# Decoder trunk on one core: kernel zeros sent later, x splits at high priority, one gate tile ahead of the GLU, and a pause between scan tiles

## The chip, the cores and the metric

The kernel runs on one core of a Trainium2 chip. The metric is the device time of one launch in microseconds, the median of the runs. TensorE is called PE here, its weight load PEld, VectorE DVE, ScalarE ACT, GpSimd POOL, and the engine that issues most transfers SP.

## The reference

Two layers are applied to x of 512 tokens by 1024 channels, in float32. Each layer projects x once and splits the columns:

```
proj = x @ w_in[l]     # 1024 -> u 512 | z_ssm 512 | q latent 256 | kv latent 128 | rotary key 32
                       #         | z_mla 512 | q_mem 512 | z_mem 512 | merge-gate logits 3 x 1024
y_ssm = glu(s5(u)) * silu(z_ssm)              # 32 groups x 64 complex states, scan over 512 tokens
y_mla = latent_attention(...) * silu(z_mla)   # 8 heads, causal, rotary part of 32
y_mem = attention(q_mem, mem) * silu(z_mem)   # 4 heads, 256 memory tokens
merged = sum_i sigmoid(gate_i) * (y_i @ p_i)  # 1024 channels
x = layer_norm(ALPHA * x + merged @ w_out[l])
glu(y): g = gelu(y); a, b = split(g @ w_glu + b_glu); a * sigmoid(b)
```

The S5 branch discretises a diagonal state matrix with a step `dt = exp(log_dt)` per group, so exponentials, sines and cosines of the parameters are needed before its scan.

## The kernel before

**Matmuls.** Everything is kept transposed, channels on partitions and the 512 tokens as columns. Float32 accuracy comes from splitting each operand into a rounded high half and a remainder: `split_to` casts the high half on ACT (L594, or L597 with a scale) and subtracts it on DVE (L595, L598). `mm3` then issues three matmuls, high by high (L97), high by low (L98) and low by high (L99). `w_in_tile` makes one 128-column tile of the input projection: two weight blocks (`wblock`: a load of 256 KB by SP, a cast, a subtract) and 24 matmuls of 512 columns. `gate2` makes of such a tile z times 1 + tanh(z/2): a tanh on ACT and a multiply on DVE.

**Order.** PE's instructions run in the order in which the Python generators issue them. A running model of PE time, `E.clk`, advanced by each `mm3`, decides when a background stream (`tick`) gets its turn. The other engines' instructions are ordered by a scheduler by priority; `tc.high_priority` moves instructions forward. Each engine executes its list strictly in order, and so does SP's list of transfers.

**Start of layer 0.** `first_tiles` loads the weights of three latent tiles and the eight tiles of x (`x(k)`), and multiplies as they arrive. `param_setup` computes on DVE `dt` by `v_exp` (some 20 small operations, L109 to L124), then on POOL the phases (`v_sincos` on `ang = ai * dt`, L299), and from these all S5 parameters; the second `v_exp` (mag) is again on DVE. POOL goes on with `s5_powers` and `s5_pool` of scan tile 0, which makes `bt`, `bm`, `cl`, `cosn` and `sinn`; POOL's tensor operations have the line of a helper, L71. Meanwhile PE makes u tile 0, u tile 1, the rotary key, `mem_values` and `mem_keys`.

**The scan stream.** `s5_stream` runs four tiles of eight groups per layer as background. `s5_tile` issues: `kp`, the convolution kernel of a block of 8 tokens (L477, L478); two transposes of `bm`; `pb` = B u; on DVE a rotation with `cosn` and `sinn` (L513 to L518), a scan (L519), and the rotation back; then `py`, a GELU, a transpose `yt` back (L540), a copy of it on ACT (L542), and two transfers through DRAM that end in `yb`. The next tile or the end of the stream splits `yb` (L597, L598 in `tail`) into one of four operands `E.g` of the GLU. `kp`, `tp`, `pb`, `py` and `yt` share one PSUM bank. The kernel tile `kt` is written into the middle of a DRAM buffer `E.kd` whose front 112 columns are zeros, so that it can be read back as a Toeplitz matrix `tz`. These zeros are stored once, at the start of the program.

**Around the stream.** In each layer the memory attention runs first (scores `sm`), then eight merge tiles of that branch, then up to four gate tiles of the S5 branch (`ZS`, each only while the stream is not done), then what is left of the stream, then `glu_tile` 0 to 2. `mla_phase` runs the eight heads of the latent attention with fill work between the steps: GLU tile 3, then for every even head the gate tile `ZA` of that pair of heads and two merge tiles. `mla_values` transposes the probabilities (L963), copies them (`pt`, L966) and multiplies by v (`av`, L971). The buffers of the pool F (five) hold the tanh results, gates and GLU intermediates.

Of the kernel before, what the change touches and what calls it, by code (L numbers as in the profile page):

```python
# [10 lines left out]
F32 = mybir.dt.float32  # L11
# [443 lines left out]
    E.uds[ut] = ud  # L455


def s5_tile(E, l, ut, t, tail):

    nc = E.nc
# [8 lines left out]
    kd = E.kd[ut % 2]  # L471
# [85 lines left out]
def s5_stream(E, l, first, period):  # L557

    base = E.clk + first
    tail = None  # L560
    for ut in range(4):
        t = E.s5t if E.s5t is not None else s5_pool(E, l, ut)
        E.s5t = None
        yield max(base + ut * period, E.clk)
        tile = s5_tile(E, l, ut, t, tail)
        while True:
            try:
                d = next(tile)
            except StopIteration as e:
                tail = e.value  # L570
                break
            yield E.clk + d
    yield E.clk + E.cfg["tok_us"]
    tail()
# [88 lines left out]
def first_tiles(E, l):  # L663

    n = 3
    ps = [pmm(E) for _ in range(n)]
    E.X = [[E.xp.tile([128, 4, 512], F32R, name="X", tag="X") for _ in range(2)] for _ in range(2)]

    def x(k):
        raw = load_raw(E, E.I["xT"][k], tag="PPPPPPFF"[k])  # L670
        split_to(E, *xpart(k), raw)

    def xpart(k):
        return tuple(a[:, k % 4, :] for a in E.X[k // 4])

    def mm(t, k):
        mm3(E, ps[t], w[t].at(cols(k % 4)), xpart(k), k == 0, k == 7)

    src = lambda t, hf: E.I["w_in"][l, Tiles.CQ + t, hf]
    w = [wblock(E, src(0, 0))]  # L680
    x(0)
    mm(0, 0)
    w.append(wblock(E, src(1, 0)))
    mm(1, 0)
    x(1)
    mm(0, 1)
    w.append(wblock(E, src(2, 0)))
    mm(1, 1)
    x(2)
    mm(2, 0)  # L690
    mm(2, 1)
    x(3)
    for t in range(n):
        mm(t, 2)
    w2 = [split(E, load_raw(E, src(t, 1), tag="S")) for t in range(n)]
    x(4)
    for t in range(n):
        mm(t, 3)
    load_params(E)
    w = w2  # L700
    for k in range(4, 8):
        if k > 4:
            x(k)
        for t in range(n):
            mm(t, k)
    return ps
# [94 lines left out]
def latents(E, l):  # L801

    nc = E.nc
    v = nc.vector
    cs, sq = [], []
    first = first_tiles(E, l) if l == 0 else None
    for i, t in enumerate((Tiles.CQ, Tiles.CQ + 1, Tiles.CKV)):
        ps = first[i] if first else (yield from w_in_tile(E, l, t))
        c = ftile(E, "c")
        v.tensor_copy(c, ps)  # L810
        s = stile(E, "sq")
        nc.scalar.activation(out=s, in_=ps, func=AF.Square)
        cs.append(c)
        sq.append(s)
    if l == 0:
        param_setup(E)
    yield from u_tile(E, l, 0)
    if l == 0:
        mem_load(E, "AAAA")
        yield from u_tile(E, l, 1)  # L820
    ss = E.psum.tile([128, 512], F32, name="ss", tag="sc")
    v.tensor_tensor(out=sq[0], in0=sq[0], in1=sq[1], op=ALU.add)
    for j in range(2):
        for t in range(4):
            nc.tensor.matmul(ss[32 * t:32 * t + 32, cols(j)], lhsT=E.ones, rhs=sq[2 * j][:, cols(t)], start=True, stop=True)
    m2, hu = stile(E, "ms"), stile(E, "hu")
    ms, rs = m2[:, 0:256], m2[:, 256:512]
    for j, n in enumerate((256, 128)):
        v.tensor_scalar(out=ms[:, cols(j)], in0=ss[:, cols(j)], scalar1=1.0 / n, scalar2=EPS, op0=ALU.mult, op1=ALU.add)
    v_rsqrt(nc, rs, ms, hu[:, 0:256], hu[:, 256:512])  # L830
    if l > 0:
        yield from u_tile(E, l, 1)
    pk = pmm(E)
    w = load_raw(E, E.I["w_kr"][l], 256)
    for k in range(2):
        for b in range(2):
            for i in range(4):
                x = (k * 4 + i) * 32
                nc.tensor.matmul(pk[32 * i:32 * i + 32, :], lhsT=w[:, x:x + 32], rhs=fl(E.X[k][b][:, i, :]),
                                 start=k + b == 0, stop=k + b == 2)  # L840
    E.ks = stile(E, "ks") if l else E.cst.tile([128, 512], F32, name="ks", tag="cs")
    nc.scalar.copy(E.ks, pk)
    E.clk += 3.4
    yield
    if l == 0:
        E.phases = s5_powers(E, l)
        next(E.phases)
        yield from mem_values(E, l)
    E.cn = []
    E.scale = scale_latents(E, l, cs, rs)  # L850
    if l > 0:
        drain(E.scale)
        rotate_key(E, rotary_sums(E))
# [140 lines left out]
def z_tile(E, l, t, box, pool=None):  # L994
    box.append(gate2(E, (yield from w_in_tile(E, l, t)), pool))
# [177 lines left out]
def run(E, gen):  # L1173
    for _ in gen:
        tick(E)
# [114 lines left out]
    run(E, f)  # L1290


def mla_phase(E, l, first, fill):

    ys, ks, vs, ws, qs, z = {}, {}, {}, {}, {}, {}

    def prepare(h):
        hp, j = h // 2, h % 2
        if j == 0:
            ks[hp] = yield from mla_k(E, l, hp)  # L1300
            ws[hp] = wblock(E, E.I["w_uq"][l, hp])
            z[hp] = []
        qs[h] = yield from mla_q(E, l, hp, j, ws[hp])
        if h in (0, 3):
            vs[(h + 1) // 4] = yield from mla_v(E, l, (h + 1) // 4)

    def values(h, Ps, f):
        hp, j = h // 2, h % 2
        if j == 0:
            ys[hp] = E.yp.tile([128, 512], F32, name="ya", tag="Y")  # L1310
        return mla_values(E, h, Ps, vs[h // 4], ys[hp], z[hp], f)

    def fills(h):
        if h >= 0 and h % 2 == 0:
            return [z_tile(E, l, Tiles.ZA + h // 2, z[h // 2])] + fill[h:h + 2]
        return [first] if h < 0 else []

    f = attention(E, HEADS, prepare, lambda h, Ps: mla_scores(E, qs[h], ks[h // 2][h % 2], Ps), values, fills, E.cfg["mla_lag"],
                  E.cfg["mla_us"], E.cfg["lace_us"])
    run(E, f)  # L1320
    E.ya = [split(E, ys[hp], 0.5) for hp in range(4)]
# [9 lines left out]
def trunk(tc, I, out):  # L1331
    nc = tc.nc
    with ExitStack() as es:
# [15 lines left out]
        E.clk, E.bg, E.bg_at, E.s5t, E.uds = 0.0, None, 0.0, None, [None] * 4  # L1349
        E.x1 = E.dram.tile([S, D], F32, name="x1", tag="x1", bufs=1)  # L1350
        es.enter_context(tc.manual_schedule(engines={mybir.EngineType.PE}))
        zk = E.s5b.tile([128, 1024], F32, name="zk", tag="tz")
        nc.gpsimd.memset(zk, 0.0)
        E.kd = []
        for i in range(2):
            E.kd.append(E.dram.tile([32, 8, 240], F32, name="kd", tag=f"kd{i}", bufs=1))
            for h in range(2):
                nc.sync.dma_start(out=E.kd[i][0:16, :, h * 56:h * 56 + 56], in_=zk[0:16, 0:448].rearrange("p (g x) -> p g x", g=8))
        for l in range(DEPTH):
            E.macc, E.mg, E.g, E.ym, E.ysm = [None] * 8, [], [], [], []  # L1360
            if l == 0:
                warm_up(E)
            run(E, latents(E, l))
            E.bg = s5_stream(E, l, CFG["s5_first"][l], CFG["s5_period"])
            E.bg_at = E.clk
            tick(E)
            if l == 0:
                for i, _ in enumerate(mem_keys(E, l)):
                    if i in E.cfg["sl"]:
                        next(E.scale, None)  # L1370
                    tick(E)
            mem_phase(E, l)
            ym = [split(E, y, 0.5) for y in E.ym]
            rope = rope_tables(E) if l == 0 else idle()
            next(rope, None)
            for m in range(8):
                run(E, merge_tile(E, l, 2, m, ym, True, False))
                if m < 4:
                    next(rope, None)
            if l == 0:  # L1380
                ps = rotary_sums(E)
                drain(rope)
                rotate_key(E, ps)
            z = [[] for _ in range(4)]
            for i in range(CFG["zs"]):
                if E.bg is not None:
                    run(E, z_tile(E, l, Tiles.ZS + i, z[i], "P"))
            while E.bg is not None:
                E.bg_at = 0.0
                tick(E)  # L1390
            run(E, chain(*[glu_tile(E, l, i, z[i]) for i in range(3)]))
            mla_phase(E, l, glu_tile(E, l, 3, z[3]), [merge_tile(E, l, 0, m, E.ysm, False, False, E.halting) for m in range(8)])
            if l + 1 < DEPTH:
                E.phases = s5_powers(E, l + 1)
                next(E.phases)
                E.s5t = s5_pool(E, l + 1, 0)
            run(E, merge_all(E, l, 1, E.ya, False, True))
            run(E, out_norm(E, l, I["x"] if l == 0 else E.x1, out if l == DEPTH - 1 else E.x1))
# [75 lines left out]
```

## Time and profile before

| | |
|---|---|
| median of 3 runs | 1124.85 us (1123.71 to 1125.21) |
| profiled execution | 1121.5 us |
| its span, first to last instruction | 1119.4 us |
| mean granted PE clock | 0.985 of full speed |
| PE / PEld / DVE / ACT / POOL busy | 95% / 76% / 62% / 45% / 45% |
| DMA | 117.97 MB, 105 GB/s |

A matmul is pipelined, so its busy time (0.39 us for 512 columns) is longer than the distance to the next one. Idle time in brackets is what an engine waited just before an instruction, with the engine and line that released it.

### The profile page before, as it was taken

What the parts mean: (1) busy time and instruction counts of PE and PEld (TensorE: products, weight loads), DVE (VectorE), ACT (ScalarE), POOL (GpSimd) and SP (SyncE); (2) the same over time, 40 slices, a digit from 0 to 9 for tenths busy, and PEclk for the clock granted to TensorE, in tenths of its full rate; (3) what the DMA queues carried; (4) which work ended last, traced back from release to release, by engine and by line L of the source; (5) the groups of instructions that cost most, each with busy time, mean ns of one, the idle gap of its engine ahead of it and who ended that gap; (6) DMA issues with size and microseconds to landing.
All of it is one profiled execution on the core that took longest, in us unless ns stands there. A gap on an engine that the chain in (4) does not pass through costs nothing.

```text
span 1119.4 us, 16046 instructions
## 1 busy us (share of the span) xinstructions
PE 1063.0 (95%) x5584; PEld 851.8 (76%) x5584; DVE 695.2 (62%) x1274; ACT 508.7 (45%) x1010; POOL 499.5 (45%) x890
## 2 busy tenths in 40 slices
PE   7979999999999999999979999899899999999995
PEld 5678777777877777888868788788788777778885
DVE  7686687964666663753586676675447565545328
ACT  4335544233576654433334355433346656543331
POOL 4998885661033334863550275581002243320163
PEclk9989999999999999999999999999999999999998
DMA  6534244253322222444544434344322222234341
GB/s 197 150 115 123 69 113 119 77 146 88 86 70 67 68 76 67 134 121 134 151 144 140 116 97 109 94 118 120 103 83 88 73 52 74 67 115 130 111 134 76
DMA packets 87665, 117.97 MB, mean 105 GB/s; under 512 B 24097, under 2 KB 36513, under 8 KB 87585
## 3 DMA queue, kind: packets, MB, share of 16 engines
q1 hardware_dynamic: 86944, 114.85, 36.4%
q0 software_dynamic: 640, 2.10, 0.7%
q8 instruction: 44, 0.72, 0.3%
q14 instruction: 37, 0.30, 0.1%
HBM read 107.37 MB, written 9.55 MB: 104 GB/s over the span
## 4 chain that ended last, share of the span: by engine, by line
PE 64%; DVE 13%; POOL 9%; DMA 7%; ACT 3%; issue 3%; SPq 1%; DVEq 0%; ACTq 0%; POOLq 0%
PE mm L97 17%; PE mm L99 17%; PE mm L98 17%; PE av L971 2%; PE tp L963 2%; DMA raw<-in_w_in 2%; DMA yb<-yd 2%; DVE w L595 2%; DMA yd<-r 2%; POOL carve L71 1%; PE py L531 1%; POOL cl L71 1%; DMA raw<-in_w_out 1%; PE sa L98 1%; PE sa L99 1%
## 5 line engine op out<-in xcount | busy, mean ns | idle before, releaser
L97 PE MATMUL mm<-X,w 128*128 128x512 f32 x740 | 298.0, 403 | 0.6 <-ACT X L594 0.5
L99 PE MATMUL mm<-X,w 128*128 128x512 f32 x740 | 290.2, 392 | 2.2 <-DVE w L595 2.1
L98 PE MATMUL mm<-X,w 128*128 128x512 f32 x740 | 289.7, 391 | 0.2 <-DVE X L595 0.2
L595 DVE TENSOR_TENSOR w<-raw,w 128x512 fp32r<-128x512 f32 (+2 forms) x247 | 206.7, 842 | 123.0 <-ACT w L594 121.5
L594 ACT CAST w<-raw 128x512 fp32r<-128x512 f32 (+1 forms) x317 | 191.5, 606 | 193.5 <-PE mm L99 89.8
L71 POOL TENSOR_TENSOR w<-raw,w 128x512 fp32r<-128x512 f32 x70 | 92.9, 1329 | 316.2 <-ACT w L594 239.3
L99 PEld LDWEIGHTS mm<-X,w 128*128 128x128 f32 x740 | 139.2, 188 | 34.2 <-DVE w L595 3.9
L97 PEld LDWEIGHTS mm<-X,w 128*128 128x128 f32 x740 | 140.3, 190 | 30.6 <-issue 2.9
L98 PEld LDWEIGHTS mm<-X,w 128*128 128x128 f32 x740 | 139.6, 189 | 27.1 <-DVE X L595 0.9
L97 PE MATMUL mm<-hl,w 128*128 128x512 f32 (+1 forms) x296 | 112.9, 382 | 4.7 <-ACT hl L597 4.7
L99 PE MATMUL mm<-hl,w 128*128 128x512 f32 (+1 forms) x296 | 111.5, 377 | 5.9 <-DVE w L595 5.9
L98 PE MATMUL mm<-hl,w 128*128 128x512 f32 (+1 forms) x296 | 111.0, 375 | 1.3 <-DVE hl L598 1.3
L99 PEld LDWEIGHTS mm<-hl,w 128*128 128x128 f32 x296 | 57.5, 194 | 16.7 <-DVE w L595 7.0
L97 PEld LDWEIGHTS mm<-hl,w 128*128 128x128 f32 x296 | 57.6, 194 | 14.2 <-ACT hl L597 5.5
L98 PEld LDWEIGHTS mm<-hl,w 128*128 128x128 f32 x296 | 57.6, 195 | 10.7 <-DVE hl L598 1.9
L1029 ACT ACTIVATE thg<-mm,bg 128x512 f32<-128x512 f32 x48 | 33.0, 687 | 59.2 <-PE mm L99 57.1
L762 ACT ACTIVATE P<-P,mx 128x256 f32<-128x256 f32 (+2 forms) x96 | 51.2, 542 | 14.2 <-DVE mx L761 13.9
L71 POOL TENSOR_TENSOR macc<-macc,thg 128x512 f32<-128x512 f32 x16 | 25.2, 1578 | 64.2 <-DVE thg L1039 64.2
L1039 DVE SCALAR_TENSOR_TENSOR thg<-thg,mm 128x512 f32<-128x512 f32 x32 | 22.0, 688 | 45.1 <-PE mm L99 44.9
L760 ACT ACTIVATE P<-sa,mx 128x128 f32<-128x128 f32 (+1 forms) x64 | 33.7, 527 | 30.5 <-DVE mx L759 29.9
L914 POOL TENSOR_SCALAR hl<-hl 32x512 fp32r<-32x512 f32 x32 | 20.3, 635 | 52.7 <-PE mm L98 35.0
L947 DVE TENSOR_TENSOR sa<-sa,mask 128x128 f32<-128x128 f32 x64 | 19.0, 297 | 31.1 <-PE sa L99 30.7
(361 smaller groups left out, 2002.8 us busy)
## 6 DMA issues: line engine op xcount, KB each, us to landing
raw<-in_w_in SPq DMA_DIRECT2D x188, 256.0 KB
raw<-in_p SPq DMA_DIRECT2D x48, 256.0 KB
raw<-in_w_mem_kv SPq DMA_DIRECT2D x32, 256.0 KB
raw<-in_w_out SPq DMA_DIRECT2D x32, 256.0 KB
tz<-kd SPq DMA_DIRECT2D x8, 512.0 KB
raw<-in_w_glu SPq DMA_DIRECT2D x16, 256.0 KB
raw<-in_xT SPq DMA_DIRECT2D x8, 256.0 KB
raw<-in_memT SPq DMA_DIRECT2D x8, 256.0 KB
```

The costliest lines, as they stand in the source:

```text
L71: ins = g.tensor_tensor(**k)
L97: t.matmul(out, lhsT=a[0], rhs=b[0], start=start, stop=False)
L98: t.matmul(out, lhsT=a[0], rhs=b[1], start=False, stop=False)
L99: t.matmul(out, lhsT=a[1], rhs=b[0], start=False, stop=stop)
L594: nc.scalar.copy(hi, src)
L595: (eng or nc.vector).tensor_tensor(out=lo, in0=src, in1=fl(hi), op=ALU.subtract)
L760: nc.scalar.activation(out=P, in_=ps, func=AF.Exp, bias=mx[:, 1:2], accum_out=mx[:, 2:3])
L762: nc.scalar.activation(out=P, in_=P, func=AF.Copy, scale=mx[:, 3:4])
L963: nc.tensor.transpose(tp[:, cols(t)], Ps[t][:, cols(kb)], E.ident)
L971: mm = lambda out, rhs, start, stop: nc.tensor.matmul(out, lhsT=w, rhs=rhs, start=start, stop=stop)
L1029: nc.scalar.activation(out=th, in_=pg, func=AF.Tanh, bias=E.bg2[:, col:col + 1], scale=0.5)
L1039: v.scalar_tensor_tensor(out=th, in0=th, scalar=1.0, in1=pp, op0=ALU.add, op1=ALU.mult)
```

## The change

Four edits. The zeros of `E.kd` are set and stored in a function of their own, called in layer 0 behind u tile 1; only the 16 x 448 part that is stored is set, on DVE where it was POOL. The splits in `x(k)` get high priority. The gate tile `ZA` + 0 of the latent attention is made between the S5 gate tiles and the rest of the stream, and `mla_phase` takes it as given. The stream lets PE's model time run 2 us on before scan tiles 1 to 3 begin.

```diff
+def kernel_zeros(E):
+    zk = E.s5b.tile([128, 1024], F32, name="zk", tag="tz")
+    E.nc.vector.memset(zk[0:16, 0:448], 0.0)
+    E.kd = []
+    for i in range(2):
+        E.kd.append(E.dram.tile([32, 8, 240], F32, name="kd", tag=f"kd{i}", bufs=1))
+        for h in range(2):
+            E.nc.sync.dma_start(out=E.kd[i][0:16, :, h * 56:h * 56 + 56], in_=zk[0:16, 0:448].rearrange("p (g x) -> p g x", g=8))
@@ s5_stream
-        yield max(base + ut * period, E.clk)
+        yield max(base + ut * period, E.clk + (2.0 if ut else 0.0))
@@ first_tiles, x(k)
-        split_to(E, *xpart(k), raw)
+        with E.tc.high_priority(E.cfg["prio"]):
+            split_to(E, *xpart(k), raw)
@@ latents
         yield from u_tile(E, l, 1)
+        kernel_zeros(E)
@@ mla_phase
-def mla_phase(E, l, first, fill):
-    ys, ks, vs, ws, qs, z = {}, {}, {}, {}, {}, {}
+def mla_phase(E, l, first, fill, z0):
+    ys, ks, vs, ws, qs, z = {}, {}, {}, {}, {}, {0: z0}
-            z[hp] = []
+            z.setdefault(hp, [])
-            return [z_tile(E, l, Tiles.ZA + h // 2, z[h // 2])] + fill[h:h + 2]
+            return ([] if z[h // 2] else [z_tile(E, l, Tiles.ZA + h // 2, z[h // 2])]) + fill[h:h + 2]
@@ trunk
-        zk = E.s5b.tile([128, 1024], F32, name="zk", tag="tz")
-        nc.gpsimd.memset(zk, 0.0)
...
+            z0 = []
+            run(E, z_tile(E, l, Tiles.ZA, z0))
             while E.bg is not None:
                 E.bg_at = 0.0
                 tick(E)
             run(E, chain(*[glu_tile(E, l, i, z[i]) for i in range(3)]))
-            mla_phase(E, l, glu_tile(E, l, 3, z[3]), [...])
+            mla_phase(E, l, glu_tile(E, l, 3, z[3]), [...], z0)
```

DVE, start of the program, before: the first exponential (`carve_320`) runs to L124, which gives `dt`, and the second follows; the subtracts of x tiles 5 to 7 (`X`), of the first u tile's weights (`w`) and of the first mem tile (`hl`) come behind.

```order
L117 SCALAR_TENSOR_TENSOR carve_320<-carve_320 128x64 x4
L118 TENSOR_TENSOR carve_320<-carve_320 128x64
L119 TENSOR_TENSOR carve_320<-carve_320 128x64
L120 TENSOR_SCALAR carve_320<-carve_320 128x64
L124 TENSOR_TENSOR carve_319<-carve_320 128x64
L301 TENSOR_TENSOR carve_319<-par0_249,carve_319 128x64
...
L595 TENSOR_TENSOR X_159<-raw_268,X_158 128x512
L120 TENSOR_SCALAR carve_320<-carve_320 128x64
L595 TENSOR_TENSOR X_159<-raw_281,X_158 128x512
L124 TENSOR_TENSOR carve_319<-carve_320 128x64
L595 TENSOR_TENSOR X_159<-raw_294,X_158 128x512
```

The same engine and place now (the subtract of `split_to` has line 606, `dt` is `carve_311`); the three subtracts of x stand just ahead of this piece, between L112 and L117 of the same first exponential.

```order
L606 TENSOR_TENSOR w_453<-raw_451,w_453 128x512
L117 SCALAR_TENSOR_TENSOR carve_312<-carve_312 128x64
L123 CAST carve_312<-carve_312 128x64
L606 TENSOR_TENSOR w_470<-raw_468,w_470 128x512
L117 SCALAR_TENSOR_TENSOR carve_312<-carve_312 128x64
L606 TENSOR_TENSOR hl_492<-raw_489,hl_491 128x512
L117 SCALAR_TENSOR_TENSOR carve_312<-carve_312 128x64 x2
L118 TENSOR_TENSOR carve_312<-carve_312 128x64
L119 TENSOR_TENSOR carve_312<-carve_312 128x64
L120 TENSOR_SCALAR carve_312<-carve_312 128x64
L124 TENSOR_TENSOR carve_311<-carve_312 128x64
```

Six large subtracts have moved from behind the first exponential's end to ahead of it.

PE, layer 0, between scan tile 0 and scan tile 1, before: `yt` of the old tile, then `kp` of the new.

```order
L98 MATMUL mm_1507<-X_159,w_1569 128x512
L99 MATMUL mm_1507<-X_158,w_1569 128x512
L540 MATMUL yt_1612<-ident_70,rb_1314 128x128 x4
L477 MATMUL kp_1625<-c0_1257,bt_1244 32x16
L478 MATMUL kp_1625<-cl_1262,bt_1244 32x112
```

The same place now (`yt` has line 551): the rows are the start of a stretch of twelve such matmuls, and `kp` follows behind the twelfth.

```order
L551 MATMUL yt_1612<-ident_70,rb_1314 128x128 x4
L97 MATMUL mm_1507<-X_150,w_1569 128x512
L98 MATMUL mm_1507<-X_151,w_1569 128x512
L99 MATMUL mm_1507<-X_150,w_1569 128x512
L97 MATMUL mm_1629<-X_148,w_1632 128x512
```

Twelve matmuls of input-projection tiles have moved between the two, and they do so at all three such places of each layer. Likewise the work between the last `yt` of a layer and the first matmul that needs the fourth operand `E.g` grows from 36 matmuls to 51 in layer 0 and 66 in layer 1.

PE, end of the latent attention in layer 0, before: the last transpose of probabilities (`tp`), twelve matmuls of a gate tile, the last value matmul, and merge work of the S5 branch.

```order
L963 MATMUL tp<-ident,P 128x128
L97 MATMUL mm<-X,w 128x512
L98 MATMUL mm<-X,w 128x512
L99 MATMUL mm<-X,w 128x512
...
L971 MATMUL av<-pt,vv 64x128
L97 MATMUL mm<-ysm,w 128x512
```

The same place now, where `tp` and `av` have lines 976 and 984.

```order
L984 MATMUL av<-pt,vv 64x128 x2
L976 MATMUL tp<-ident,P 128x128
L984 MATMUL av<-pt,vv 64x128
L97 MATMUL mm<-X,w 128x512
L98 MATMUL mm<-X,w 128x512
```

The last value matmul has come to stand directly behind the last transpose, in both layers, and the remaining S5 merge work is done before it.

## Rows read from the trace of the kernel before

**Rows 1.** The page's first part: busy us, share of the span, instructions.

```profile
PE 1063.0 (95%) x5584; PEld 851.8 (76%) x5584; DVE 695.2 (62%) x1274; ACT 508.7 (45%) x1010; POOL 499.5 (45%) x890
```

**Rows 2.** Waits of PE: who waited for whom, us in total, times, longest.

```profile
PE kp L477 <- ACT r L542: 6.7, 6, 2.2
PE mm L98 <- DVE X L595: 4.6, 2, 4.4
PE av L971 <- ACT pt L966: 2.7, 6, 0.6
...
PE kp L478 <- POOL cl L71: 0.6, 1, 0.6
```

**Rows 3.** Windows: length, busy us and instructions by engine, PE clock, DMA.

```profile
core 0: us, PE busy (x) PEld busy (x) DVE busy (x) ACT busy (x) POOL busy (x), PEclk, DMA share, GB/s
...
150.00:180.00 30.00, 27.72 (x148) 22.24 (x147) 29.25 (x46) 10.39 (x18) 19.47 (x26) 0.94 0.25 71
270.00:282.00 12.00, 9.48 (x34) 7.09 (x33) 3.80 (x5) 3.63 (x6) 0.00 (x0) 0.86 0.29 84
480.00:510.00 30.00, 30.00 (x134) 24.85 (x133) 18.03 (x22) 11.16 (x19) 13.37 (x24) 1.00 0.41 120
804.00:816.00 12.00, 8.54 (x30) 6.37 (x30) 3.09 (x4) 3.92 (x6) 0.00 (x0) 0.86 0.30 88
```

**Rows 4.** Timeline, 9 to 23 us, five engines: start, duration, instruction, idle before.

```profile
9.66 0.96 POOL L1353 MEMSET zk<- 128x1024 f32 x1 [6.58 <-DVE mask L256]
...
10.65 2.61 SPq L1358 DMA_DIRECT2D kd<-zk  x4
...
16.68 0.62 ACT L594 CAST X<-raw 128x512 fp32r<-128x512 f32 x1 [4.72 <-DMA raw<-in_xT]
...
17.08 0.22 DVE L124 TENSOR_TENSOR carve<-carve 128x64 f32<-128x64 f32 x1
...
17.38 0.35 POOL L71 TENSOR_TENSOR carve<-par,carve 128x64 f32<-128x64 f32 x1 [4.98 <-DVE carve L124]
...
21.33 0.83 DVE L595 TENSOR_TENSOR X<-raw,X 128x512 fp32r<-128x512 f32 x1
...
22.21 0.80 PE L98 MATMUL mm<-X,hl 128*128 128x512 f32 x1 [4.36 <-DVE X L595]
```

**Rows 5.** Timeline, 102 to 113 us, POOL, DVE and PE.

```profile
102.21 1.61 POOL L71 TENSOR_TENSOR sinn<-sinn,tm 128x512 f32<-128x512 f32 x1
...
103.86 0.69 DVE L513 TENSOR_TENSOR rb<-pb,sinn 64x512 f32<-64x512 f32 x1 [0.77 <-POOL sinn L71]
...
112.00 0.67 DVE L598 SCALAR_TENSOR_TENSOR hl<-mm,hl 128x512 fp32r<-128x512 f32 x1
...
112.73 0.39 PE L99 MATMUL sm<-hl 128*128 128x256 f32 x1 [0.60 <-DVE hl L598]
```

**Rows 6.** Durations: a DVE group to 30 us, the zero memset, two POOL operations.

```profile
L595 DVE TENSOR_TENSOR X<-raw,X 128x512 fp32r<-128x512 f32 x8 | 5.7, 709 | 1.0 <-ACT X L594 1.0
...
L657 DVE MEMSET zero<- x1: 485/485/485, 1.3 to 1.3; 128x512 uint32 x1
...
51.97 0.28 POOL L71 TENSOR_TENSOR carve<-carve 128x64 f32<-128x64 f32 x1
...
54.29 0.90 POOL L71 TENSOR_TENSOR pwt<-LI,LR 128x64 f32<-128x64 f32 x1
```

**Rows 7.** Timeline of PE, 132 to 138 us: the second kernel tile.

```profile
136.07 0.25 PE L477 MATMUL kp<-c,bt 128*32 128x16 f32 x5 [2.20 <-ACT r L542]
```

**Rows 8.** Timeline of PE at the GLU starts of both layers.

```profile
276.17 0.50 PE L97 MATMUL mm<-hl,w 128*128 128x512 f32 x1 [1.86 <-ACT hl L597]
277.33 0.50 PE L98 MATMUL mm<-hl,w 128*128 128x512 f32 x1 [0.66 <-DVE hl L598]
...
809.29 0.49 PE L97 MATMUL mm<-hl,w 128*128 128x512 f32 x1 [2.81 <-ACT hl L597]
810.43 0.79 PE L98 MATMUL mm<-hl,w 128*128 128x512 f32 x1 [0.65 <-DVE hl L598]
```

More of the change, by code (lines that the diff above doesn't have):

```diff
@@ L1351, in trunk @@
         es.enter_context(tc.manual_schedule(engines={mybir.EngineType.PE}))
-        zk = E.s5b.tile([128, 1024], F32, name="zk", tag="tz")
-        nc.gpsimd.memset(zk, 0.0)
[L1354 to L1358, printed above, removed]
         for l in range(DEPTH):
@@ L1391, in trunk @@
             run(E, chain(*[glu_tile(E, l, i, z[i]) for i in range(3)]))
-            mla_phase(E, l, glu_tile(E, l, 3, z[3]), [merge_tile(E, l, 0, m, E.ysm, False, False, E.halting) for m in range(8)])
+            mla_phase(E, l, glu_tile(E, l, 3, z[3]), [merge_tile(E, l, 0, m, E.ysm, False, False, E.halting) for m in range(8)], z0)
             if l + 1 < DEPTH:
```

## The prediction

> **What bounds the kernel now.** I read the engine totals first [rows 1]: TensorE (PE) is busy 95% of the span, so only its idle time and its slow-clock time can be won, about 56 us of idle. In steady work 134 matmuls of 512 columns take 30.0 us, 0.224 us each [rows 3], and that is the price of one matmul used as cover below. Second, PE's list of waits [rows 2]: the change touches three entries, the wait for the low half of x (4.6 us), the kernel tile `kp` that waits for ScalarE's copy of `yt` (6.7 us over six times), and, at the start of the GLU, the split of the fourth scan result [rows 8]. Third, the windows with the granted clock [rows 3]: around both GLU starts the mean clock is 0.86 over 12 us, so 12 x 0.14 = 1.7 us of full speed is lost at each, at the lower of the two levels. Fourth, the timeline at both ends of the one long GpSimd (POOL) computation [rows 4, 5], because a wait that goes at 22 us is worth something only if nothing later holds the engine back to its old time.
>
> **Part 1: x splits first, kernel zeros later (start to 113 us).** Before, the low half of x tile 5 stands behind two exponentials on VectorE (DVE), starts at 21.33 though ScalarE cast the high half at 16.68, and PE waits 4.36 us [rows 4]. Now the three late subtracts stand inside the first exponential. The four zero stores (2.61 us of SP's queue [rows 4]) no longer stand ahead of the three x loads, which are issued some 2.5 us earlier; the wait goes completely. The stores now stand between the mem loads, and what is queued behind them there (three mem loads, then the weights of the second u tile) loses at most those 2.61 us of issue. The zeros are written long before the first kernel store. The memset on POOL (0.96 us, in its idle stretch before 17.38) goes for nothing; the one on DVE has fewer columns than the memset of 0.485 us in [rows 6], so it costs between nothing and that; I take 0.5.
>
> So PE gains 4.4 us at 22 us, and the clock drop behind that wait with it (1.7 us by the price above). But it doesn't keep them. POOL begins its chain (phases, powers, the matrices of scan tile 0) when `dt` is finished, that is behind L124 of the first exponential: 17.38, and before that it waited 4.98 us for it [rows 4]. From there it works without a gap worth naming to the end of `sinn` at 103.82. DVE stands 0.77 us at L513 for `sinn`; DVE then works without a gap until it finishes the low half of a query at 112.67, and PE's score matmul waits 0.60 us for that [rows 5]. The order of these instructions is the same after the change. What PE gained before this place is therefore lost in this one wait, except 0.6 us; and if POOL starts later, PE is later than before.
>
> It does start later. In the new order six subtracts of 128x512 (three of x, two of the first u tile's weights, one of mem) stand ahead of the L124 that releases POOL; before they stood behind it. At a mean of 0.709 us [rows 6] that is 4.3 us; the memset adds 0.5; the casts of x now ahead of two weight casts add about 0.3 (half a cast of 0.62 [rows 4]). Their loads come 2.5 us earlier, so I count no wait for them. POOL starts 5.1 us later. Part of this returns. POOL's 128x64 operation takes between 0.28 and 0.90 us in the same chain [rows 6], and the long ones are those that meet DVE's large operations; six of these now run before POOL starts, worth between 0 and 6 x 0.62 = 3.7 us. I take half, 1.9. So at 112.7 PE is 5.1 - 1.9 = 3.2 us late, after a wait of about 9 us in place of 0.60.
>
> The Trainium skill, page "SBUF — State Buffer", section "SBUF: two separate sides", says that VectorE and GpSimd share one port pair as an exclusive lock held for a whole instruction, and that a VectorE operation with two SBUF inputs takes it. By that rule each of the six subtracts could hold POOL for its full 0.7 us, 4.2 us in all; PE would be only 0.9 us late at 112.7 and the sum 2.3 us lower. The rows with 0.28 and 0.90 us agree in kind, but by them a meeting costs POOL at most 0.62 us.
>
> Behind a wait of 9 us I also expect the clock to drop once, as it did behind the GLU waits of 2 to 3 us: 1.7 us more. Part 1: +3.2 + 1.7 = **+4.9 us**. Its ends: -0.6 (POOL not late, no drop) and +8.5 (nothing returned, two drops).
>
> **Part 2: the pause between scan tiles.** `kp` of tiles 1 to 3 of each layer uses the one PSUM bank that ScalarE must first empty of `yt`. In the example ScalarE is held by softmax work and PE waits 2.20 us [rows 7], the longest of the six [rows 2]. The new order puts 12 matmuls between, 12 x 0.224 = 2.7 us, in all six places. So the 6.7 us go, and 0.6 of waiting for POOL's `cl` too [rows 2]. What is displaced is other PE work that was due anyhow, and the next scan tile starts some 2.7 us later. **-7.3 us**; the bounds are 0 (DVE was the true limit around some of them; see the rivals) and -7.3.
>
> **Part 3: the gate tile ahead of the GLU.** Between the last `yt` and the first matmul that needs the fourth scan result stood, before, 36 matmuls in either layer (27 and 9 more of the first three results); now 51 in layer 0 and 66 in layer 1. The added 15 cover 3.4 us and the added 30 cover 6.7; the waits are 1.86 + 0.66 and 2.81 + 0.65 us [rows 8]. All 5.98 go, and both drops of the clock (3.4 us) with them. In layer 0 only 0.9 us of cover is left over. On ScalarE and DVE the split of the scan result stands ahead of the new tile's tanh and multiply, so it does not queue behind them. **-9.4 us**; if the chain of two transfers comes late again, -6.
>
> What was fill inside the latent attention is now 24 matmuls shorter. The remainder shows at its end: before, 12 matmuls stood between the last transpose and the last value matmul, now none. PE then waits for the copy of `pt`. The largest such wait in the trace is 0.6 us, with 12 matmuls of cover in most [rows 2]; a bare one lies between 0.6 and the 1.9 us that ScalarE's copy needed at the GLU [rows 8]. I take 0.6 twice, **+1.2 us**. The gate tile also holds one of five F buffers through the GLU; I count nothing, since its four other buffers carry two GLU tiles.
>
> **Sum**: +4.9 - 7.3 - 9.4 + 1.2 = -10.6 us. The profiled execution took 1121.5 us, which becomes 1110.9; the median of the runs is 3.35 us higher, so 1124.85 - 10.6 = **1114.2 us**.
>
> **The rivals.**
> - *The front gain stays.* If POOL's chain is not what holds 112.7 us (its contention fell so far, or DVE's order lets PE through), PE keeps 4.4 + 1.7 us: -6.1 - 7.3 - 9.4 + 1.2 = -21.6, 1103.2 us. For it: PE really stood on a DVE queue there [rows 4]. Against it: 0.77 us of DVE waiting for `sinn` and 0.60 of PE waiting for DVE are both in the row [rows 5]. If only the late start is wrong (part 1 at -0.6) it is 1108.8.
> - *The pauses buy nothing.* From 150 to 180 us DVE is busy 29.25 of 30 us [rows 3]; where DVE is the limit, a wait for ScalarE that goes comes back as a wait for DVE. Then part 2 is 0: -3.3, 1121.6 us. For it that row; against it, only one or two of the six places lie in such a stretch.
> - *Slower: the F buffers.* With the gate's result held, `gl` and `gt` of a third GLU tile need buffers that the first frees only after its multiply by z. If ScalarE stands there, PSUM is not emptied and PE stops at each of the eight GLU tiles: at 1.9 us, the length of the wait in [rows 8], 15 us, +4.6 in the sum, 1129 us. It decides from the point where a GLU tile's evacuation takes over two tiles of PE work, 48 x 0.224 = 10.8 us. Against it: DVE and ScalarE operations of about 0.7 us, six of them for a tile, make some 4 us.
> - *The change does nothing at the GLU* if the pauses push the stream's end as far back as the gate tile adds cover. The counts above (51 and 66 against 36) already hold both, so I give this no chance of its own.
>
> **How the numbers follow.** Forecast 0.63, front gain stays 0.15, pauses buy nothing 0.15, slower 0.07. The forecast's own range runs from -16 (part 1 at -0.6) to -5 (part 1 at +8.5, a third of part 2 lost): 1109 to 1120. To leave out no more than 2 in 10 with the rivals: 1105 to 1121 us. Within 0.2% (2.2 us, about what a measurement can tell) is 1122.6 to 1127.1. Faster: 0.63 x 0.97 + 0.15 + 0.15 x 0.7 = 0.87; same 0.06; slower 0.07.
>
> **What would show it.** In the profile after: PE's wait for x near 22 us gone; POOL's first L71 near 22 us instead of 17.38; DVE at L513 waiting several us for `sinn`, and PE's score matmul behind it some 9 us, ending at 114 to 118 (this makes part 1 right; a wait under 1 us there makes it wrong); no `kp` wait for ScalarE over 0.3 us; no wait and clock 1.00 at both GLU starts; two short waits for `pt` at the ends of the attentions. A time under 1105 would say that POOL did not bind, one over 1121 that covered waits came back on DVE.

## The result and the profile after

| | before | changed |
|---|---|---|
| median of 4 runs | 1124.32 us | 1113.28 us (1111.52 to 1115.11) |
| ratio | 1 | 0.9882, 95% interval 0.9846 to 0.9918 |
| profiled execution, span | 1121.5, 1119.4 us | 1111.52, 1109.5 us |

1114.2 us was forecast. The total is met; the parts show why, and that two of them were wrong in opposite directions. First the page's engine totals of the changed kernel (busy us, share, instructions).

```profile
PE 1059.8 (96%) x5584; PEld 849.9 (77%) x5584; DVE 680.2 (61%) x1275; ACT 507.0 (46%) x1010; POOL 497.8 (45%) x889
```

PE runs the same 5584 matmuls as in [rows 1]. Of the 9.9 us that the span lost, its idle time gave 6.7 and its busy time 3.2. The waits of PE in the changed kernel (who waited for whom, us in total, times, longest) show which went and which are new.

```profile
PE kp L489 <- POOL cl L71: 8.6, 2, 8.0
PE tp L976 <- ACT P L774: 4.8, 4, 2.6
PE tx L1117 <- DVE mv L181: 4.1, 1, 4.1
PE av L984 <- ACT pt L979: 3.5, 8, 0.7
PE sm L97 <- ACT hl L608: 3.5, 1, 3.5
PE yt L551 <- DVE rb L547: 3.0, 1, 3.0
PE sm L99 <- DVE hl L609: 2.7, 3, 1.5
```

The wait of `kp` for ScalarE and that for the low half of x [rows 2] are not in the list any more, nor are the GLU's [rows 8]. In their place stand `kp` for `cl` (GpSimd), `sm`, `yt` for a VectorE product, and `tp` for the softmax rows `P`.

The timeline of the changed kernel at the front (start, duration, instruction, idle before):

```profile
21.27 0.36 POOL L71 TENSOR_TENSOR carve<-par,carve 128x64 f32<-128x64 f32 x1 [7.61 <-DVE carve L124]
...
84.15 0.39 PE L489 MATMUL kp<-cl,bt 128*32 128x112 f32 x1 [7.98 <-POOL cl L71]
...
106.83 0.69 DVE L524 TENSOR_TENSOR rb<-pb,sinn 64x512 f32<-64x512 f32 x1 [6.06 <-POOL sinn L71]
...
113.34 0.58 PE L97 MATMUL sm<-hl 128*128 128x256 f32 x1 [3.48 <-ACT hl L608]
115.59 0.58 PE L99 MATMUL sm<-hl 128*128 128x256 f32 x1 [1.46 <-DVE hl L609]
```

GpSimd starts 3.9 us later than in [rows 4], VectorE gets the sine product 2.97 us later than in [rows 5], and PE pays for it in two places, at `kp` and at `sm`. The windows of the changed kernel (length, busy us and instructions by engine, PE clock, DMA) show the clock behind both waits, and the stretches of [rows 3].

```profile
76.00:91.00 15.00, 6.43 (x47) 4.72 (x47) 2.78 (x8) 2.82 (x9) 14.57 (x35) 0.66 0.19 59
110.00:122.00 12.00, 7.20 (x25) 5.87 (x26) 10.96 (x19) 5.96 (x16) 11.92 (x22) 0.72 0.23 64
150.00:180.00 30.00, 29.64 (x168) 24.36 (x167) 27.53 (x36) 11.81 (x20) 25.84 (x33) 1.00 0.37 94
272.00:284.00 12.00, 12.00 (x55) 9.91 (x54) 4.21 (x6) 4.65 (x9) 0.00 (x0) 1.00 0.40 109
480.00:510.00 30.00, 30.00 (x134) 24.85 (x133) 18.29 (x22) 11.16 (x19) 11.86 (x20) 1.00 0.41 120
800.00:812.00 12.00, 12.00 (x56) 9.95 (x55) 2.96 (x5) 3.62 (x6) 0.00 (x0) 1.00 0.45 131
```

The mean clock is 0.66 and 0.72 behind the two new waits: the lower of the two levels for most of the time there. At the GLU, in the last window and the one from 272 us, PE is never idle and the clock is full.

To place gains and losses where the order of the matmuls differs, I set the traces beside each other at equal PE work: every matmul counts with the steady distance to the next one, by columns (about 0.23 us for 512, 0.12 for 256, and so on), and the table gives how much later (+) or earlier (-) than the kernel before a kernel has done the same work. Each column is one profiled execution. "Front alone" is the kernel before with the late zeros and the early splits of x only, and so on; the last two columns have the pauses and the gate tile, but not the front.

```
work done before at | changed | front  | pause | gate  | without | three S5
                    |         | alone  | alone | alone | front   | gate tiles
 30 us (x done)     |   -5.3  |  -4.5  |  +1.4 |  +0.2 |   +1.1  |  +1.2
 80 us              |  -13.7  | -13.1  | +13.9 |  +0.3 |   +0.2  | +13.6
130 us (scan 0)     |   +4.9  |  +5.6  | +14.5 |  +0.2 |   +0.7  | +14.3
270 us (GLU)        |   -2.2  |  +6.2  |  +7.3 |  +0.3 |   -6.6  |  +7.2
320 us (attention)  |   -7.1  |  +6.4  | +10.9 |  -4.7 |  -11.5  |  +2.5
480 us (its end)    |    0.0  |  +6.4  | +18.1 |  -2.5 |   -4.4  |  +5.1
640 us (layer 1)    |   -1.0  |  +7.5  | +18.6 |  -1.7 |   -5.0  |  +5.4
800 us (GLU)        |   -6.0  |  +7.0  | +13.5 |  -1.9 |   -9.3  |  +0.4
820 us              |  -11.1  |  +6.8  |  +8.3 |  -7.4 |  -14.4  |  -4.7
1080 us             |   -9.9  |  +6.8  | +10.1 |  -6.1 |  -13.2  |  -2.5
```

In the changed kernel the front ends at +4.9, the pauses bring 7.1 us in layer 0 and 5.0 in layer 1, the GLU starts 4.9 and 5.1, and the attention of layer 0 loses 7.1.

### The profile page after: what moved, and what is told of

Its sections match the earlier page's. It is cut to its first block, busy times and chain, and to the rows that moved or that the text cites. A ratio compares the mean times of both kernels' runs of the same rounds, so it can differ in the third digit from the quotient of the medians.

```text
span 1109.5 us, 16056 instructions
## 1 busy us (share of the span) xinstructions
PE 1059.8 (96%) x5584; PEld 849.9 (77%) x5584; DVE 680.2 (61%) x1275; ACT 507.0 (46%) x1010; POOL 497.8 (45%) x889
## 4 chain that ended last, share of the span: by engine, by line
PE 71%; DVE 10%; POOL 8%; ACT 3%; DMA 3%; issue 3%; SPq 0%; DVEq 0%; ACTq 0%; POOLq 0%
PE mm L97 19%; PE mm L99 19%; PE mm L98 19%; PE av L984 2%; PE tp L976 2%; POOL carve L71 1%; PE py L542 1%; PE pb L518 1%; DVE w L606 1%; ACT w L605 1%; DMA yb<-yd 1%; DMA yd<-r 1%; PE sa L98 1%; PE sa L99 1%; DVE mv L185 1%
## 5 line engine op out<-in xcount | busy, mean ns | idle before, releaser
L606 DVE TENSOR_TENSOR w<-raw,w 128x512 fp32r<-128x512 f32 (+1 forms) x247 | 196.8, 802 | 123.8 <-ACT w L605 122.3
L97 PE MATMUL mm<-hl,w 128*128 128x512 f32 (+1 forms) x296 | 111.5, 377 | 0.2
L99 PE MATMUL mm<-hl,w 128*128 128x512 f32 (+1 forms) x296 | 109.3, 369 | 0.1
L98 PE MATMUL mm<-hl,w 128*128 128x512 f32 (+1 forms) x296 | 109.1, 369 | 0.3 <-DVE hl L609 0.3
L97 PEld LDWEIGHTS mm<-hl,w 128*128 128x128 f32 x296 | 56.5, 191 | 9.7 <-DVE z L726 1.1
L99 PEld LDWEIGHTS mm<-hl,w 128*128 128x128 f32 x296 | 56.0, 189 | 10.0 <-DVE w L606 0.3
L98 PEld LDWEIGHTS mm<-hl,w 128*128 128x128 f32 x296 | 56.1, 190 | 9.1 <-DVE hl L609 0.8
```

The costliest lines, as they stand in the source:

```text
L97: t.matmul(out, lhsT=a[0], rhs=b[0], start=start, stop=False)
L98: t.matmul(out, lhsT=a[0], rhs=b[1], start=False, stop=False)
L99: t.matmul(out, lhsT=a[1], rhs=b[0], start=False, stop=stop)
L606: (eng or nc.vector).tensor_tensor(out=lo, in0=src, in1=fl(hi), op=ALU.subtract)
```

## The experiments

All times are ratios to the kernel before on the same chip. The kernel before itself spread from 1119.6 to 1135.0 us over these runs, and an interval is some 0.2 to 0.5% either way. One kernel that was run on two chips came to 0.9847 and 0.9913, so differences under 0.7% between chips say little; the mechanisms are read from the traces. The intervals:

| kernel | ratio | 95% interval |
|---|---|---|
| changed, again | 0.9929 | 0.9907 to 0.9950 |
| front alone | 0.9999 | 0.9970 to 1.0027 |
| pause alone | 0.9961 | 0.9924 to 0.9998 |
| gate tile alone | 0.9950 | 0.9917 to 0.9984 |
| pause and gate, no front; again | 0.9847; 0.9913 | 0.9808 to 0.9886; 0.9874 to 0.9952 |
| changed, x at normal priority | 0.9905 | 0.9885 to 0.9925 |
| no front, GELU at high priority | 0.9866 | 0.9844 to 0.9888 |
| no front, gate tiles shifted | 0.9900 | 0.9870 to 0.9930 |
| no front, two memsets | 0.9951 | 0.9921 to 0.9981 |
| no front, three S5 gate tiles | 0.9885 | 0.9835 to 0.9934 |
| the last, rotary tables later | 0.9911 | 0.9880 to 0.9941 |

### The parts alone

Front alone: the changed kernel without these two edits.

```diff
-        yield max(base + ut * period, E.clk + (2.0 if ut else 0.0))
+        yield max(base + ut * period, E.clk)
-            run(E, z_tile(E, l, Tiles.ZA, z0))
```

> Kernel before plus the early splits of x and the late zeros only. Theory 1 (the prediction's part 1: the long GpSimd computation starts late and binds until 113 us): 1124.3 + 4.9 = 1129.2 us; GpSimd's first product with dt near 21 us, VectorE waits about 6 us at L524 for the last sine product. Rival 2 (the front gain stays): 1124.3 - 6.1 = 1118.2 us. Rival 3 (only the slow clock behind the wait costs, which the pauses or the gate tile brought): no difference, 1124 us.

The trace agrees with theory 1: GpSimd's first product at 22.04 us, +5.6 us at 130. The time does not: no difference, and 4.9 us lie just outside the interval. Rival 2, a lasting gain, is out by both. Rival 3 has the time right and the reason wrong, since the waits and the slow clock are there in this kernel too. A likely reason for the disagreement is in the section on the hardware. Of the nine other traces with the front of the kernel before, five lose time at this very place to a VectorE subtract that stands for over 12 us; the one trace of the kernel before does not, so for its timed runs this is inferred. At 130 us the four traces with the zeros sent late stand at +4.9, +5.6, +7.8 and +9.3 us (mean 6.9), the ten others between 0 and +14.5 (mean 5.7). In the two of the four that have such a subtract GpSimd delivers the last `cl` only 0.2 and 0.5 us later than in the kernel before, and PE waits neither for it nor for the sine product: the cost of the front is seen only where the subtract does not stand.

Pause alone (the changed line of `s5_stream` in the kernel before, nothing else):

> Kernel before plus the pause of 2.0 us between scan tiles only. Theory 1 (the prediction's part 2: six waits for ScalarE's copy go, nothing else): 1124.3 - 7.3 = 1117.0 us. Theory 2, from setting both traces beside each other at equal PE work (layer 0 gained 6.9 us and layer 1 5.0 us between the front and the GLU): 1124.3 - 11.9 = 1112.4 us. Rival 3 (covered waits come back as waits for VectorE): 1124 us.

The table reads -7.2 us from 130 to 270 us and -5.1 from 640 to 800: theory 2's place and size. The profiled execution was 1132.2 us, since it lost 14 us at 50 to 75 us. It lost 7.2 more in the attention of layer 0, though this kernel has all its gate tiles there (2.7 of them at 480 us, at a wait of 2.2 us for VectorE that is 0.3 in the changed kernel), and 3.6 at the first GLU, where only 27 matmuls of cover are left and PE waits 4.7 us. The timed runs, -0.4%, allow theory 1 and exclude theory 2 as totals. They don't speak for theory 1's mechanism: from 130 us to the end the table, too, gives only -4.4 us, because these losses take back most of what the scan gained.

Gate tile alone (the `z0` lines in the kernel before):

> Kernel before plus the gate tile ahead of the GLU only. Theory 1 (the prediction's part 3: -9.4 at the GLU starts, +1.2 at the ends of the latent attention): 1116.1 us. Theory 2, from the two traces at equal PE work (-9.6 at the GLU starts, but +7 in the latent attention of layer 0 and +1.2 in that of layer 1, because its first head has lost 24 matmuls of fill): 1124.3 - 1.4 = 1122.9 us. Should the 7 us in layer 0 belong to the pauses or the front instead, the latent attention here shows no wait for P over 1 us and theory 1's time holds.

Theory 1, within its interval: -5.0 and -5.5 at the GLU, +2.2 and +1.3 in the attentions, no wait for `P` over 0.3 us. So the 7 us are not the gate tile's, and theory 2 falls.

The front undone:

```diff
-        with E.tc.high_priority(E.cfg["prio"]):
-            split_to(E, *xpart(k), raw)
+        split_to(E, *xpart(k), raw)
-        kernel_zeros(E)
```

(with the zeros again at the start of `trunk`)

> Changed kernel with the front undone (zeros first, splits of x at normal priority), pauses and gate tile kept. Theory 1 (the front costs 4.9 us in this company too): 1113.3 - 4.9 = 1108.4 us, GpSimd's first product with dt back at 17.4 us. Rival 2 (the front gain stays): 1113.3 + 6.1 = 1119.4 us.

GpSimd starts at 18.22 us, near the 17.38 of before, and PE is at +0.7 instead of +4.9 at 130 us; 1108.2 us in the profile. It was run twice, with the changed kernel again between:

> The changed kernel once more, beside the kernel before on the chip of these runs, to set the price of the front: the kernel without the front came to 0.9847 of the time before. Theory 1 (the front costs 4.9 us): 0.9847 + 0.0044 = 0.989, about 1114 us for 1126. Rival (the front costs nothing or gains): 0.985 or less.

> Kernel with pauses and gate tile, without the front, once more as the base of the next two. Theory 1 (front costs 4.9 us): 0.985 of the time before, against 0.988 to 0.993 measured with the front. Theory L (one VectorE subtract that GpSimd's products of scan tile 0 sometimes lock out for some 14 us at 60 to 75 us is what spreads the times of every kernel here): the runs fall into two clusters near 1108 and 1114 us, and a profile with a subtract over 10 us there belongs to the upper one.

0.9847 and 0.9913 without the front, 0.9882 and 0.9929 with it: a difference of 0.35 and 0.16% in theory 1's favour, both smaller than an interval. The fastest runs are 1107.35 without it and 1111.52 in the changed kernel, 4.2 us apart; but the front alone and the kernel before have 1121.42 and 1119.62, only 1.8 apart. That the front costs 4 to 6 us where VectorE is not locked out is read from one trace of each kernel; what it costs on average stays open between 0 and 5 us. Theory L is borne out in part. In the second set without the front three runs lie at 1107 to 1110 us and nine at 1115 to 1123 us, with a gap of 4.9 us between. The profile at 1114.8 has a subtract of 13.98 us, that of the first set at 1108.2 none over 2.9. But the upper runs are spread over 8.6 us and not near 1114, so one subtract doesn't explain them all.

### Priority or zeros

> Changed kernel without the high priority of the splits of x; the zeros are still sent late. In the order of VectorE the six large subtracts stand ahead of L124 here as in the changed kernel. Theory 1 (the early loads, not the priority, put the subtracts there and so delay GpSimd): GpSimd's first product with dt near 21 us, the wait of kp for cl near 8 us again, same time as the changed kernel, 0.989. Rival (the priority is what delays it): GpSimd's product at 17.4 us and 0.985.

The timeline of this kernel for GpSimd:

```profile
22.09 0.35 POOL L71 TENSOR_TENSOR carve<-par,carve 128x64 f32<-128x64 f32 x1 [8.75 <-DVE carve L124]
```

Late without any priority: sending the zeros late is enough to bring six subtracts in front of L124. I read it as the work of the four stores that leave SP's queue ahead of x; the memset that moved to VectorE with them was not separated. The wait of `kp` for `cl` was missed: `kp` waited for nothing here, since PE itself had lost 11.0 us to a VectorE subtract before it got there.

### The wait for P

Where the changed kernel loses 7.1 us, its timeline shows the softmax of the first head meeting the end of GLU tile 3:

```profile
312.42 1.44 DVE L609 SCALAR_TENSOR_TENSOR ysm<-gl,ysm 128x512 fp32r<-128x512 f32 x1
...
320.75 0.69 ACT L772 ACTIVATE P<-sa,mx 128x512 f32<-128x512 f32 x1 [0.84 <-DVE mx L771]
321.76 0.72 ACT L774 ACTIVATE P<-P,mx 128x512 f32<-128x512 f32 x1 [0.23 <-DVE mx L773]
322.53 0.33 PE L976 MATMUL tp<-ident,P 128*128 128x128 f32 x1 [2.63 <-ACT P L774]
```

First I moved the remaining gate tiles one pair of heads forward, so that the first head has its 24 matmuls again:

```diff
-            return ([] if z[h // 2] else [z_tile(E, l, Tiles.ZA + h // 2, z[h // 2])]) + fill[h:h + 2]
+            n = h // 2 + 1
+            z[n] = []
+            return ([z_tile(E, l, Tiles.ZA + n, z[n])] if n < 4 else []) + fill[h:h + 2]
```

> Kernel without the front (pauses and gate tile kept), with the gate tiles of the latent attention each made one pair of heads earlier, so that the first head has 24 matmuls of fill again and the last pair none. Theory 1 (the two waits for P, 2.6 and 1.8 us, and what follows them come from the gate tile that is missing at the first head, so that the S5 merge tiles run there): the waits for P go, the latent attention of layer 0 takes 141 to 143 us instead of 147.3 for the same matmuls, and the time falls by 4 to 6 us, to 0.980. Rival (the scan pauses alone bring these waits, by what they leave in front of the attention): the waits stay and the time is that of the kernel without the front, 0.985.

The 1.8 us wait went, the first stayed at 2.3, and the loss from 320 to 480 us fell only from 7.1 to 5.3. That theory falls for the larger part, and the rival points to the pauses. They push the stream's end behind the fourth S5 gate tile, which `trunk` makes only while the stream is not done: in layer 0, 105 matmuls on `hl` (the GLU's and those of the first keys and queries) now precede the first score in place of 93, and GLU tile 3 ends in the first head. Next kernel: three S5 gate tiles and two of the attention's.

```diff
+            z0, z1 = [], []
+            run(E, z_tile(E, l, Tiles.ZA, z0))
+            run(E, z_tile(E, l, Tiles.ZA + 1, z1))
-    ys, ks, vs, ws, qs, z = {}, {}, {}, {}, {}, {0: z0}
+    ys, ks, vs, ws, qs, z = {}, {}, {}, {}, {}, {0: z0, 1: z1}
-CFG: zs=4
+CFG: zs=3
```

> Kernel without the front, with three instead of four S5 gate tiles made ahead and two gate tiles of the latent attention instead of one, so that in layer 0 the fourth S5 gate tile is again fill at the start of the latent attention, with the same cover at the start of the GLU. Theory Z (the pauses moved this tile ahead of the stream's end, and that is why the first head's softmax chain meets the end of the GLU tile and PE waits 2.6 and 1.8 us for P): both waits go, 4 to 6 us less in layer 0, 0.980 of the time before; the second pair of heads loses 24 matmuls of fill and may give back 1.2 us in each layer. Rival (the chain itself is too slow for the cover in any order): the waits for P stay or move, 0.985.

Waits of PE from 310 to 490 us, first with the pause alone, then in this kernel from 320 us:

```profile
PE tp L974 <- ACT P L773: 2.3, 1, 2.3
PE mm L98 <- DVE hl L609: 2.2, 1, 2.2
PE av L982 <- ACT pt L977: 0.9, 3, 0.6
```

```profile
PE av L982 <- ACT pt L977: 1.8, 4, 0.5
PE tp L974 <- ACT P L773: 1.1, 2, 0.6
```

No wait is over 0.6 us, and the attention of layer 0 now loses 2.6 us against the kernel before, not 7.1. Theory Z's mechanism holds. Its time, 0.980, was not met: 0.9885 is told apart neither from the changed kernel nor from its own base, 0.9913 on the same chip. Its profile starts 14 us behind for the reason in the last section and still ends 2.5 ahead; its fastest run, 1103.58 us, is the fastest of all kernels.

### The wait of yt

> Kernel without the front, with the four operations of the scan's GELU at high priority. Theory 1 (in the second scan tile the pauses turned a wait for ScalarE into one for VectorE: yt waits 3.2 us for a GELU product that stands behind the sine work of the rotary tables): that wait falls under 1 us and with it the slow clock behind it, 3.2 + 1.7 = 4.9 us at best, 0.980; at least 1.5 us, as DVE's two products at the end of that stretch stand behind only some small operations. Rival (DVE is the limit there and something else waits instead): no difference, 0.985.

`yt` still waits 3.02 us. The order of VectorE did not change: the GELU's first product (L546) still runs behind the sine work, over 7 us after ScalarE's square (L545) that it needs. Why the priority did not move it was not found. The time is the rival's, but not its reason. This kernel's timeline, ScalarE, GpSimd and VectorE:

```profile
170.61 0.60 ACT L545 ACTIVATE r<-py 128x512 f32<-128x512 f32 x1 [2.07 <-PE py L542]
...
170.66 2.56 POOL L71 TENSOR_TENSOR cl<-c,LR 128x1024 f32<-128x1024 f32 x1 [0.94 <-PE py L542]
...
171.46 4.75 DVE L132 SCALAR_TENSOR_TENSOR carve<-carve 128x64 f32<-128x64 f32 x4
...
178.40 0.68 DVE L546 SCALAR_TENSOR_TENSOR r<-r,py 128x512 f32<-128x512 f32 x1
```

Four operations that take 0.23 us each elsewhere take 4.75 us beside GpSimd's products, which start when `py` releases `cl`. So I took the sine work away from there (on top of the three S5 gate tiles):

```diff
-            next(rope, None)
-                if m < 4:
+                if m >= 3:
                     next(rope, None)
```

> The kernel of the last comparison (pauses, three S5 gate tiles and two gate tiles of the latent attention ahead of the GLU, no front), with the sine work of the rotary tables begun three merge tiles later. Theory (yt of the second scan tile waits 3.2 us because GpSimd's products of cl lock VectorE out of four small sine operations at 171 to 176 us, and the GELU products stand behind these in VectorE's order): the GELU products no longer stand behind the sine work, the yt wait falls under 0.5 us and the slow clock behind it goes, 3.2 + 1.7 = 4.9 us less than that kernel at equal luck in front; the fastest runs near 1099 us, ratio about 0.984 where that kernel had 0.9885. Rival (VectorE is the limit of the whole stretch from 150 to 240 us): the wait comes back at the third scan tile, where the sine work now stands, and the ratio stays near 0.9885.

PE in this kernel:

```profile
188.44 0.60 PE L551 MATMUL yt<-ident,rb 128*128 128x128 f32 x4
...
261.58 1.12 PE L359 MATMUL tp<-ident,carve 128*128 128x128 f32 x4 [5.73 <-DVE carve L354]
```

The first half of the theory holds: no wait of `yt`, and 170 to 190 us gives 1.1 us where the other kernel lost 3.9. But the tables are now late for their own transposes, and PE waits 5.7 us at 261 with a mean clock of 0.81 from 250 to 268 us. No gain is left: 0.9911, and the fastest run is 1111.01 us where 1099 was expected. A smaller shift was not tried.

## Why the prediction was right, and where not

- **Part 1, +4.9 us: the chain that binds was right, the size was right in undisturbed executions** (+4.9 in the changed kernel, +5.6 with the front alone), **and in part by luck.** GpSimd started 3.9 us late (5.1 predicted) and VectorE's sine product was 3.0 us late (3.2). The 0.9 us between the two did not come back in the way I gave, by six subtracts that run before GpSimd starts: that term, 1.9, is not in the rows. GpSimd's lateness grew to 7.7 us at the last `bm` product, and fell to 3.1 by 91 us, while PE stood at `kp` and VectorE was busy 1.12 of 11 us. First the kernel before, then the changed kernel, and a window of the latter:

```profile
69.52 1.65 POOL L71 TENSOR_TENSOR bm<-bm,tb 128x512 f32<-128x512 f32 x1
```

```profile
77.23 1.65 POOL L71 TENSOR_TENSOR bm<-bm,tb 128x512 f32<-128x512 f32 x1
...
80.00:91.00 11.00, 6.26 (x44) 4.65 (x45) 1.12 (x5) 2.33 (x8) 10.57 (x30) 0.58 0.05 13
```

  I read both moves as contention with VectorE: GpSimd's `tb` product of 128x512 takes 1.48 us at 72.6 and 1.05 at 80.8. Two details failed as well. PE gave its lead back first at `kp`, for `cl`, 8.6 us, and only then at `sm`, 5; I had looked for the end of GpSimd's chain and not at its middle product. And the lead was 13.7 us, not 4.4, since the w splits of the memory tiles at 60 to 75 us were late no longer either. Two stretches of slow clock came, at 79 and 113 us; what the first cost went into the wait at `sm`, and only the second counts. By timed runs the cost is smaller than this, or none.
- **Part 2, -7.3 us: the mechanism right, the size too small.** All six waits for ScalarE went; the table gives -12.1. The unnamed part: three waits for VectorE, of 2.1, 1.8 and 1.8 us before 165, 204 and 701 us, went too. In the profile with the pause alone 0.4 us of the first is left and nothing of the others; with the gate tile alone all three are there. They are among these waits of the kernel before:

```profile
PE mm L99 <- DVE w L595: 8.0, 7, 1.8
...
PE av L98 <- DVE hl L595: 2.1, 1, 2.1
...
PE av L97 <- DVE ym L797: 1.8, 1, 1.8
```

  I read this as the scan's rotations moving 2.7 us behind the splits that PE waited for; it was not tested. The rival "the pauses buy nothing" was right at one place of six: at 185 us the `yt` wait of 3.0 us is a covered wait that came back on VectorE.
- **Part 3 at the GLU, -9.4 us: right,** -10.0 in the changed kernel (4.9 and 5.1), -10.5 with the gate tile alone, clock 1.00 at both.
- **Part 3's +1.2 us at the attention: the step that failed.** It measured +8.3 (7.1 and 1.2). I let only the gate tile's fill shrink and looked at the attention's end; the pauses took another 24 matmuls from its beginning in layer 0, by the condition on the stream in `trunk`. The prediction noted that the cover counts "already hold both" and did not ask from where the added matmuls came. With the gate tile alone it is 2.2 and 1.3 us in the two layers.
- A gain of 1.0 us at the change of layers is no term of mine. The sum, -10.6, stands against -9.9 in the profile and -11.0 in the medians. It is right because the errors cancel: -4.8 in part 2, -0.6 at the GLU and -1.0 between the layers against +7.1 in the attention.
- The F buffers never bound: no wait of PE at the GLU tiles, and two gate tiles held instead of one cost none either.

## What to carry to other kernels

When work is pulled forward to cover a wait, count what it leaves behind in every phase that used it as fill, and find the conditions ("only while the stream runs") that move whole tiles when something else shifts. A wait removed ahead of a long chain on another engine is worth what the chain's first link gains, and may cost if the same edit delays that link. Compare two orders at equal work done, not at equal time; it separates the parts of a change in one table.

## What the runs showed of the hardware

One VectorE subtract of 128x512, 0.7 us as a rule, can stand for 14 us while GpSimd works. The changed kernel's second profile, VectorE, GpSimd and PE:

```profile
66.66 13.95 DVE L606 TENSOR_TENSOR w<-raw,w 128x512 fp32r<-128x512 f32 x1
```

```profile
66.20 0.84 POOL L71 TENSOR_TENSOR btw<-btw,btmp 128x128 f32<-128x128 f32 x1
66.99 0.09 POOL L77 MEMSET halt<- 128x1 f32 x1
67.04 1.92 POOL L71 TENSOR_TENSOR bm<-bt,LR 128x1024 f32<-128x1024 f32 x1
...
78.81 1.25 POOL L71 TENSOR_TENSOR cl<-cl,tb 128x512 f32<-128x512 f32 x1
80.01 0.09 POOL L77 MEMSET halt<- 128x1 f32 x1
80.06 0.65 POOL L71 TENSOR_TENSOR pwt<-ES 128x32 f32<-128x32 f32 x1
```

```profile
80.66 0.58 PE L99 MATMUL mm<-hl,w 128*128 128x256 f32 x1 [10.28 <-DVE w L606]
```

Ten products of GpSimd, from `bm` to `cl`, go by before the subtract ends during the next small operation, though tiny memsets stand between them. Of 14 profiles, seven have such a subtract of 12.2 to 14.1 us between 60 and 81 us, one has 6.4, and six have none over 3.1. The same code fell on either side: without the front PE was at +0.7 in one profile and +6.4 in the other at 130 us (1108.2 and 1114.8 us in the end), with all edits at +4.9 and +7.8 (1111.5 and 1114.4). So executions with it are 3 to 14 us behind at 130 us. That it makes a good part of the scatter of the timed runs is likely and not shown, since only one run of each set has a trace; what decides it was not found. In all seven it ends in the same operation, the first small product behind the last `cl`; no run took GpSimd's products away to show that they are the cause.

The Trainium skill, page "SBUF — State Buffer", section "SBUF: two separate sides", has VectorE and GpSimd hold a shared port pair for a whole instruction each. These rows agree that one stands still while the other works. A loser that waits for one instruction would stand 1.9 us here, by the longest product; this one stood for ten in a row, and it was VectorE that stood, not GpSimd as the prediction's sentence on that rule had it.

I tried to give VectorE a wider opening, a second memset behind each large product:

```diff
+        if twice:
+            with self.E.tc.issue_after(m.ins):
+                g.memset(self.t[:, 8 + i:9 + i], 0.0)
```

> Kernel without the front, with two instead of one tiny memset on GpSimd behind each of its products of 512 columns or more. Theory L (a VectorE instruction gets its turn only in such a memset, and in some executions misses one after the other): with twice the opening no VectorE subtract between 55 and 80 us takes over 4 us and the upper cluster near 1114 us goes; GpSimd's chain grows by about 16 x 0.05 = 0.8 us, so 1108 to 1110 us in nearly all runs. Rival (the lockout does not depend on the length of the opening): two clusters as before, 1 us later.

```profile
62.98 6.36 DVE L610 TENSOR_TENSOR w<-raw,w 128x512 fp32r<-128x512 f32 x1
```

6.36 us in the one profile, and a time 0.4% above that of the same kernel with one memset, within the intervals. All twelve runs lie from 1113 to 1127 us, not at 1108 to 1110: no gain, and the theory of the missed openings is neither shown nor out.
